# A decoder layer on one core: the first gate and up chunks of the second feed-forward in row form, and seven buffers of converted weights

## The chip, the cores and the metric

The kernel runs on one core of one Trainium2 chip. The metric is the device time of one execution in microseconds (us), from the first to the last instruction and the little that lies around them. Engines are named as the profile names them: PE is TensorE (matmuls and transposes), ACT is ScalarE, DVE is VectorE, POOL is GpSimd, SP is SyncE, which issues nearly all DMAs here.

## The reference

One layer over 256 tokens of width 1024, batch 1: a half feed-forward, a token mixer, a cross-attention to 256 memory tokens, and a second half feed-forward. Each sub-layer normalizes its input, and its output once more before it is added to the residual stream `x`.

```python
def rmsnorm(x, g):
    xf = x.astype(jnp.float32)
    r = lax.rsqrt(jnp.mean(xf * xf, axis=-1, keepdims=True) + RMS_EPS)
    return (xf * r).astype(x.dtype) * g

def swiglu(h, w_gate, w_up, w_down):
    return (jax.nn.silu(h @ w_gate) * (h @ w_up)) @ w_down
...
        h = rmsnorm(x, xa_pre_g[l])
        mem_n = rmsnorm(mem, mem_g[l])
        c = memory_cross_attention(h, mem_n, xa_wq[l], xa_wkv[l], xa_wo[l])
        x = x + rmsnorm(c, xa_post_g[l])

        h = rmsnorm(x, ffn2_pre_g[l])
        f = swiglu(h, ffn2_w_gate[l], ffn2_w_up[l], ffn2_w_down[l])
        x = x + MACARON_WEIGHT * rmsnorm(f, ffn2_post_g[l])
```

The hidden width of the feed-forward is 2816, which is 22 chunks of 128.

## The kernel before

**Products.** Every large product is made of three matmuls on numbers split in a high part (`hi`, rounded for TensorE) and the rest (`lo`): hi by hi, hi by lo, lo by hi. Weights come from HBM in units of 8 tiles of 128 by 128 in the order of use. `Weights._make` converts one unit: ACT casts it to `whi` (L76), DVE subtracts to get `wlo` (L77). `whi` and `wlo` have six buffers each (LEAD + 2), the raw units three buffers of two units. `get` hands out tiles and converts LEAD = 4 units ahead, unless a list `pace` says otherwise for the next units.

**Two forms.** In the column form a tile of weights is the stationary operand and all 256 tokens stream past: the output has features on partitions. `group` is that form for four columns at once, 8 steps k of 12 matmuls of 256 columns (L227, L232, L234). In the row form 128 tokens are the stationary operand and 512 columns of weights stream past: the output has tokens on partitions (`row_product`, L294 to L296).

**The end of a sub-layer (a seam).** `row_end` makes the last three k-steps of the output product (`products`): first the tile of tokens t = 0 in two halves of 512 columns, then t = 1. ACT squares each half (L320), takes the root (L334), DVE inverts it (L335) and adds the normalized half to the residual `xt` (L343). PE then transposes `xt` (L349), 128 by 128 at a time; ACT and DVE split each transposed chunk into the next sub-layer's input, `x_hi` (L370) and `x_lo` (L374). Within a PSUM buffer ACT's and DVE's reads take turns in the order of the program. There are three seams: from the first feed-forward to the mixer, from the mixer to the cross-attention, and from there to the second feed-forward. The first two have fillers, columns of the memory keys (L173 to L175), which PE works on while ACT and DVE finish the tile t = 1; then the next sub-layer's `group` begins. The third has none: `ahead` and `before` thread the transposes of t = 1 through the steps of the `group` that makes the first two gate and up chunks. In a seam all engines follow the written order; outside of it only PE does, and a scheduler orders the others.

**After the third seam.** Chunks 2 to 21 of the feed-forward follow in column form, `gate_up`, with gate in one of the six `acc` buffers of PSUM and up in one of the two `sm` buffers. Between the gate and the up product of chunk 4, `opened` spreads the norm's factors over the partitions: two matmuls into an `sm` buffer (L282, four records in the trace), copied by ACT to `rBx` (L358). Then the chunks made so far are scaled, passed through Silu and split (`finish`). ACT loads a function table when it changes between Sqrt, Exp and Silu.

Of the kernel before, what the change touches and what calls it, by code (L numbers as in the profile page):

```python
# [47 lines left out]
class Weights:  # L48
# [33 lines left out]
    def open_in_parts(self, n_units, load, split):  # L82
# [21 lines left out]
        for c, (raw, hi, lo, parts) in enumerate(steps):  # L104
# [32 lines left out]
def build(nc, io, tiles_only=False):  # L137
# [171 lines left out]
    def row_sums(parts, ks, ws, t, factor, later=None):  # L309
# [54 lines left out]
    def row_end(parts, ks, weights, factor, nxt, pre, fillers):  # L364
# [12 lines left out]
        def products():  # L377
            st["w"].pace = [(LEAD, None)] * (LATE - 1) + [(LEAD - 1, None)]
# [9 lines left out]
            box["sums"] = row_sums(parts, ks, ws, 1, factor, box["later"])  # L388
            x_turn(0, range(4), small)
            x_turn(0, range(4, 8), small)  # L390

        def middle():
            r = box["r"] = row_root(box["sums"])
            if not fillers:
                x_hi(0, 0)
                row_add(1, slice(0, P), r)
                x_hi(0, 1)
                return
            for c in range(ND):
                x_hi(0, c)  # L400
            for i in range(2):
                row_add(1, quarter(i), r)
            box["later"][0]()
            for i in range(2, 4):
                row_add(1, quarter(i), r)
            for c in range(4):
                x_lo(0, c)
# [13 lines left out]
        def ahead():  # L421
            r = box["r"]
            x_turn(1, (0,), accum)
            row_add(1, slice(P, S), r)
            x_lo(0, 0)
            x_turn(1, (1,), accum)
            x_hi(1, 0)
            x_hi(1, 1)
            row_add(1, quarter(1), r)
            x_lo(1, 0)  # L430
            x_lo(0, 1)
            x_lo(1, 1)
            box["later"][0]()

        def before(j):
            if fillers and j == 1:
                k_flush()
            if j == 0 and not fillers:
                st["w"].pace = [(2, "dve"), (2, "pool"), (2, "dve"), (3, "dve"), (3, None), (3, None)]
            if j % 2 == 1 and j < 7 and not fillers:  # L440
                c = j + 1
                x_turn(1, (c, c + 1), accum)
# [662 lines left out]
```

## Time and profile before

| what | us |
|---|---|
| median of 3 runs (lowest to highest) | 579.35 (579.27 to 583.17) |
| the profiled execution | 579.55 |
| its span, first to last instruction | 577.6 |
| PE busy | 566.6 (98%) |
| DVE busy | 406.4 (70%) |
| ACT busy | 342.0 (59%) |
| mean granted TensorE clock, share of 2.4 GHz | 0.996 |

Matmuls are pipelined: the time from the start of one to the start of the next is what it costs, and the duration that a row shows is longer than that. A timeline's row has start, duration, engine, line, operation, output and input tiles, a count where rows are merged, and in brackets the idle time before it with what ended it.

### The profile page before, as it was taken

The numbers are of one execution on the slowest core, as the hardware profiler recorded it, in microseconds if no ns is written. First come the engines' busy times: TensorE is split into PE (matmuls) and PEld (weight loads), VectorE is DVE, ScalarE is ACT, GpSimd is POOL, SyncE is SP. The second block draws the span as 40 slices with busy tenths as digits, with TensorE's granted clock in tenths as the row PEclk, the third lists the DMA queues.
The fourth block names the chain that finished last, engine by engine and source line by source line (L and its number), as shares of the span: only waits on it lengthen the run. The fifth ranks groups of instructions, "written<-read, shape, count | busy, mean of one in ns | idle before, by whom it ended". The sixth has DMA issues, their size and how long they took to land.

```text
span 577.6 us, 8466 instructions
## 1 busy us (share of the span) xinstructions
PE 566.6 (98%) x3288; PEld 494.8 (86%) x3288; DVE 406.4 (70%) x661; ACT 342.0 (59%) x619; POOL 20.0 (3%) x36
## 2 busy tenths in 40 slices
PE   8999999999999999999999999999999999999995
PEld 7888888888888899988899988889888888888884
DVE  5499666778776768985578676468796666676654
ACT  6588675555556565874459466358664555555433
POOL 0000000000000000550000000010000000000001
PEclk9999999999999999999999999999999999999998
DMA  8896575465564247163347625417475455646402
GB/s 270 338 359 220 216 279 216 151 214 166 200 203 165 107 163 280 70 222 142 146 146 253 222 73 164 152 49 266 173 254 195 169 208 162 214 155 210 146 0 74
DMA packets 29832, 107.04 MB, mean 185 GB/s; under 512 B 2144, under 2 KB 3936, under 8 KB 29408
## 3 DMA queue, kind: packets, MB, share of 16 engines
q1 hardware_dynamic: 29360, 105.29, 51.4%
q10 hardware_dynamic: 432, 1.20, 0.6%
q8 instruction: 26, 0.43, 0.3%
q14 instruction: 14, 0.11, 0.1%
HBM read 105.44 MB, written 1.05 MB: 184 GB/s over the span
## 4 chain that ended last, share of the span: by engine, by line
PE 91%; DVE 3%; DMA 3%; ACT 1%; issue 1%; SPq 1%; DVEq 0%; ACTq 0%
PE acc L559 13%; PE sm L559 13%; PE acc L294 10%; PE acc L295 10%; PE acc L296 10%; PE acc L558 6%; PE sm L558 6%; DMA wraw<-w 3%; PE acc L173 3%; PE acc L174 3%; PE acc L175 3%; PE acc L234 2%; PE acc L232 2%; PE acc L260 2%; PE acc L262 2%; PE acc L261 2%
## 5 line engine op out<-in xcount | busy, mean ns | idle before, releaser
L77 DVE TENSOR_TENSOR wlo<-wraw,whi 128x1024 fp32r<-128x1024 f32 x183 | 223.9, 1231 | 84.2 <-ACT whi L76 83.8
L76 ACT CAST whi<-wraw 128x1024 fp32r<-128x1024 f32 x184 | 192.4, 1052 | 54.7 <-PE acc L296 41.4
L559 PE MATMUL acc<-xs,whi 128*128 128x512 f32 x320 | 114.5, 397 | 0.0
L559 PE MATMUL sm<-xs,whi 128*128 128x512 f32 x320 | 114.3, 397 | 0.0
L558 PE MATMUL acc<-xs,wlo 128*128 128x256 f32 x320 | 89.9, 281 | 0.7 <-DVE wlo L77 0.7
L558 PE MATMUL sm<-xs,wlo 128*128 128x256 f32 x320 | 90.0, 281 | 0.0
L559 PEld LDWEIGHTS sm<-xs,whi 128*128 128x128 f32 x320 | 60.1, 188 | 14.8
L559 PEld LDWEIGHTS acc<-xs,whi 128*128 128x128 f32 x320 | 60.1, 188 | 14.3
L294 PE MATMUL acc<-whi,h 128*128 128x512 f32 x176 | 69.7, 396 | 0.0
L295 PE MATMUL acc<-wlo,h 128*128 128x512 f32 x176 | 69.5, 395 | 0.0
L296 PE MATMUL acc<-whi,h 128*128 128x512 f32 x176 | 69.3, 394 | 0.0
L558 PEld LDWEIGHTS acc<-xs,wlo 128*128 128x128 f32 x320 | 60.4, 189 | 2.5 <-DVE wlo L77 1.1
L558 PEld LDWEIGHTS sm<-xs,wlo 128*128 128x128 f32 x320 | 60.5, 189 | 0.0
L173 PE MATMUL acc<-xs,wlo 128*128 128x256 f32 x160 | 46.1, 288 | 0.0
L175 PE MATMUL acc<-xs,whi 128*128 128x256 f32 x160 | 45.2, 283 | 0.0
L174 PE MATMUL acc<-xs,whi 128*128 128x256 f32 x160 | 45.2, 283 | 0.0
L563 ACT COPY cmb<-sm 128x256 f32<-128x256 f32 x40 | 14.9, 372 | 48.4 <-PE sm L559 48.4
L563 ACT COPY cmb<-acc 128x256 f32<-128x256 f32 x40 | 14.9, 372 | 48.1 <-PE acc L559 47.9
L296 PEld LDWEIGHTS acc<-whi,h 128*128 128x128 f32 x176 | 33.0, 187 | 8.1
L295 PEld LDWEIGHTS acc<-wlo,h 128*128 128x128 f32 x176 | 33.0, 188 | 7.8
L294 PEld LDWEIGHTS acc<-whi,h 128*128 128x128 f32 x176 | 33.0, 188 | 6.6
L232 PE MATMUL acc<-xs,whi 128*128 128x256 f32 x128 | 33.6, 292 | 1.0 <-ACT whi L108 1.0
(174 smaller groups left out, 892.5 us busy)
## 6 DMA issues: line engine op xcount, KB each, us to landing
wraw<-w SPq DMA_DIRECT2D x91, 1024.0 KB, 4.8
post<-post SPq DMA_DIRECT2D x4, 512.0 KB, 4.7
wraw<-w SPq DMA_DIRECT2D x7, 256.0 KB, 4.4
wraw<-w SPq DMA_DIRECT2D x2, 512.0 KB, 5.8
xt<-xt ACTq DMA_DIRECT2D x1, 1024.0 KB, 7.3
y<-memt SPq DMA_DIRECT2D x1, 1024.0 KB, 7.8
y<-mem SPq DMA_DIRECT2D x1, 1024.0 KB, 6.9
y<-x SPq DMA_DIRECT2D x7, 128.0 KB, 4.2
```

Of the source, the lines that this page charges most:

```text
L76: self.nc.scalar.copy(hi, raw)
L77: eng.tensor_tensor(lo, raw, hi.bitcast(F32), op=ALU.subtract)
L173: nc.tensor.matmul(o, lo, X[:, :S], start=first, stop=False, skip_group_check=True)
L174: nc.tensor.matmul(o, hi, X[:, :S], start=False, stop=False, skip_group_check=True)
L175: nc.tensor.matmul(o, hi, X[:, S:], start=False, stop=last, skip_group_check=True)
L232: nc.tensor.matmul(o[i], hi, st[X][:, k, :S], start=first and i % 2 == 0, stop=False, skip_group_check=True)
L294: nc.tensor.matmul(o, a, hi, start=first, stop=False, skip_group_check=True)
L295: nc.tensor.matmul(o, a, lo, start=False, stop=False, skip_group_check=True)
L296: nc.tensor.matmul(o, b, hi, start=False, stop=last, skip_group_check=True)
L558: nc.tensor.matmul(ps[:, S:], lo, x[:, :S], start=k == 0, stop=False, skip_group_check=True)
L559: nc.tensor.matmul(ps, hi, x, start=False, stop=k == ND - 1, skip_group_check=True)
L563: nc.scalar.copy(c, ps[:, S:])
```

## The change

It does four things.

1. In the second feed-forward the first two gate and two up chunks are made in row form by `row_group`: 24 matmuls of 512 columns for the tokens t = 0, then 24 for t = 1. All four units of their weights are taken at the start. `row_h` applies the factor, Silu and the product with token rows, and four transposes in `turn_h` bring the result to features on partitions; they stand in `opened`, behind the spread.
2. In all three seams the eight transposes of the tile t = 0 move into the last half of `products`, four behind the first k-step and four behind the second, with three `x_hi` behind the first four.
3. `early` and `late` take the place of `ahead` and the threaded steps: they order ACT's and DVE's work and the transposes of t = 1 around the steps k of the row group. The one conversion on POOL is gone, and `ahead` of `Weights` converts three units between the steps of t = 1.
4. Seven buffers of `whi` and `wlo` instead of six; the reserved memory for descriptors written by an engine is cut to 1024 bytes (no DMA is issued by POOL).

```diff
+    def ahead(self, n):
+        while self.made <= min((self.pos - 1) // UNIT + n, self.n_units - 1):
+            self._make(self.made)
+            self.made += 1
...
             for j, (k, w) in enumerate(zip(ks, ws)):
                 row_product(parts(k), st["acc"], 0, False, j == len(ks) - 1, t, d, w)
+                if (i, j) in between:
+                    between[i, j]()
...
-            box["sums"] = row_sums(parts, ks, ws, 1, factor, box["later"])
-            x_turn(0, range(4), small)
-            x_turn(0, range(4, 8), small)
+            box["sums"] = row_sums(parts, ks, ws, 1, factor, box["later"],
+                                   {(1, i): lambda i=i: turn_first(i) for i in range(2)})
+
+        def turn_first(i):
+            x_turn(0, range(4 * i, 4 * i + 4), small)
+            if i == 0:
+                for c in range(3):
+                    x_hi(0, c)
...
         def middle():
+            if fillers:
+                r = row_root(box["sums"])
+                for c in range(3, ND):
+                    x_hi(0, c)
...
+                return
             for c in range(4):
-                x_lo(0, c)
+                x_lo(0, c) if c < 3 else (x_hi(0, c), x_lo(0, c))
+            box["r"] = row_root(box["sums"])
...
+        def early(k):
+            r = box["r"]
+            if k == 0:
+                for c in range(4, ND):
+                    x_hi(0, c)
+                for i in range(2):
+                    row_add(1, quarter(i), r)
+                x_lo(0, 4)
+                box["later"][0]()
+                for c in range(5, ND):
+                    x_lo(0, c)
+                for i in range(2, 4):
+                    row_add(1, quarter(i), r)
...
+            if k == 6:
+                x_turn(1, range(4), small)
...
+        def late(k):
+            if k == 0:
+                x_turn(1, range(4, 8), small)
...
+            if k in (1, 3, 5):
+                st["w"].ahead(k // 2 + 1)
...
+                for t, ahead in enumerate((early, late)):
+                    for k, (hi, lo) in enumerate(ws):
+                        ahead(k)
+                        a = st[X][:, k, t * P:(t + 1) * P]
+                        b = st[X][:, k, S + t * P:S + (t + 1) * P]
+                        nc.tensor.matmul(ps[t], a, hi, start=k == 0, stop=False)
+                        nc.tensor.matmul(ps[t], a, lo, start=False, stop=False)
+                        nc.tensor.matmul(ps[t], b, hi, start=False, stop=k == ND - 1)
...
         def opened():
             x_spread()
+            if n == 2:
+                turn_h()
...
-              tc.tile_pool(name="hi", bufs=LEAD + 2) as hi,
-              tc.tile_pool(name="lo", bufs=LEAD + 2) as lo,
+              tc.tile_pool(name="hi", bufs=LEAD + 3) as hi,
+              tc.tile_pool(name="lo", bufs=LEAD + 3) as lo,
```

PE at the end of the first seam's `products`, before. L294 to L296 are the three matmuls of a row product, `h` is the hidden layer, L173 is the first filler:

```order
L296 MATMUL acc<-whi,h 128x512
L294 MATMUL acc<-whi,h 128x512
L295 MATMUL acc<-wlo,h 128x512
L296 MATMUL acc<-whi,h 128x512
L349 MATMUL sm<-const,xt 128x128 x8
L173 MATMUL acc<-xs,wlo 128x256
```

The same place of the change, where L300 to L302 are the row product and L357 is the transpose:

```order
L302 MATMUL acc<-whi,h 128x512
L357 MATMUL sm<-const,xt 128x128 x4
L300 MATMUL acc<-whi,h 128x512
L301 MATMUL acc<-wlo,h 128x512
L302 MATMUL acc<-whi,h 128x512
L357 MATMUL sm<-const,xt 128x128 x4
L300 MATMUL acc<-whi,h 128x512
L301 MATMUL acc<-wlo,h 128x512
L302 MATMUL acc<-whi,h 128x512
L179 MATMUL acc<-xs,wlo 128x256
```

The eight transposes stood behind the last product and now stand ahead of its last two k-steps; the other two seams have the same rows.

ACT ahead of and in the first seam, before: L579 is the Silu of chunk 21, L188 the cast of its hidden layer, L615 the load of the Sqrt table, L320 the squares and L334 the root:

```order
L76 CAST whi<-wraw 128x1024
L579 ACTIVATE gu<-gu 128x256
L76 CAST whi<-wraw 128x1024
L188 CAST h<-gu 128x256
L615 ACT_TABLE_LOAD
L76 CAST whi<-wraw 128x1024
L320 ACTIVATE q,fs<-acc 128x512 x2
L334 ACTIVATE fs<-fs 128x1
L320 ACTIVATE q,fs<-acc 128x512 x2
L334 ACTIVATE fs<-fs 128x1
```

The same place of the change, where L683 loads the Sqrt table, L602 is Silu's, L328 the squares and L342 the root:

```order
L76 CAST whi<-wraw 128x1024
L683 ACT_TABLE_LOAD
L602 ACT_TABLE_LOAD
L602 ACTIVATE gu<-gu 128x256
L76 CAST whi<-wraw 128x1024
L194 CAST h<-gu 128x256
L328 ACTIVATE q,fs<-acc 128x512 x2
L342 ACT_TABLE_LOAD
L342 ACTIVATE fs<-fs 128x1
L328 ACTIVATE q,fs<-acc 128x512
L378 ACTIVATE xs<-sm,gain 128x128 x3
L328 ACTIVATE q,fs<-acc 128x512
```

The load of the Sqrt table moved ahead of the last Silu, so that Silu's table is loaded again behind it, and Sqrt's once more between the squares and the first root.

PE between gate and up of chunk 4 in the second feed-forward, before, where L558 and L559 are the products:

```order
L558 MATMUL acc<-xs,wlo 128x256
L559 MATMUL acc<-xs,whi 128x512
L282 MATMUL pb<-const,rcx 128x128 x2
L558 MATMUL sm<-xs,wlo 128x256
L559 MATMUL sm<-xs,whi 128x512
```

And in the change:

```order
L581 MATMUL acc<-xs,wlo 128x256
L582 MATMUL acc<-xs,whi 128x512
L288 MATMUL pb<-const,rcx 128x128 x2
L649 MATMUL ht<-const,hrow 128x128 x4
L581 MATMUL sm<-xs,wlo 128x256
L582 MATMUL sm<-xs,whi 128x512
```

The four transposes `ht` came in behind the spread `pb`. Both take one of the two `sm` buffers, so that the up product behind them gets the buffer of `pb`.

## Rows read from the trace of the kernel before

**Rows 1.** The page's first part, PE: busy time, share of the span, instructions.
```profile
PE 566.6 (98%) x3288; PEld 494.8 (86%) x3288; DVE 406.4 (70%) x661; ACT 342.0 (59%) x619; POOL 20.0 (3%) x36
```
**Rows 2.** The waits of PE: for whom, us in total, times, longest.
```profile
PE acc L349 <- DVE xt L343: 0.9, 1, 0.9
...
PE acc L234 <- DVE xs L374: 0.5, 2, 0.3
```
**Rows 3.** The stretches, third seam: us; PE, PEld, DVE, ACT, POOL busy; PE clock.
```profile
381.21:396.15 14.94, 13.84 (x114) 13.31 (x112) 10.01 (x26) 12.01 (x32) 2.40 (x1) 1.00 0.20 72
```
**Rows 4.** The chain that ended last, in the first seam: start, us, what.
```profile
195.40 0.03 ACT q L320
...
196.65 0.88 DVE xt L343 x2
...
202.35 1.31 DVE xs L374 x5
```
**Rows 5.** The timeline of PE, first seam.
```profile
188.67 0.39 PE L296 MATMUL acc<-whi,h 128*128 128x512 f32 x1
...
193.81 0.39 PE L294 MATMUL acc<-whi,h 128*128 128x512 f32 x1
...
195.20 1.03 PE L349 MATMUL sm<-const,xt 128*128 128x128 f32 x8
195.99 0.37 PE L173 MATMUL acc<-xs,wlo 128*128 128x256 f32 x1
196.19 0.28 PE L174 MATMUL acc<-xs,whi 128*128 128x256 f32 x1
...
203.71 0.39 PE L234 MATMUL acc<-xs,whi 128*128 128x256 f32 x1 [0.25 <-DVE xs L374]
```
**Rows 6.** The timeline of PE, third seam.
```profile
379.84 0.39 PE L294 MATMUL acc<-whi,xs 128*128 128x512 f32 x1
...
381.21 1.03 PE L349 MATMUL sm<-const,xt 128*128 128x128 f32 x8
```
**Rows 7.** The timeline of DVE, third seam.
```profile
378.84 1.41 DVE L343 SCALAR_TENSOR_TENSOR xt<-y,fs,xt 128x512 f32<-128x512 f32 x2
```
**Rows 8.** The timeline of ACT, end of the first feed-forward and first seam.
```profile
181.73 1.05 ACT L76 CAST whi<-wraw 128x1024 fp32r<-128x1024 f32 x1
183.05 0.42 ACT L579 ACTIVATE gu<-gu 128x256 f32<-128x256 f32 x1 [0.27 <-DVE gu L576]
184.20 1.05 ACT L76 CAST whi<-wraw 128x1024 fp32r<-128x1024 f32 x1 [0.74 <-PE acc L296]
...
191.21 0.60 ACT L320 ACTIVATE q<-acc 128x512 f32<-128x512 f32 x1 [1.42 <-PE acc L296]
```
**Rows 9.** The timeline of DVE, the same place.
```profile
186.43 0.42 DVE L189 TENSOR_TENSOR h<-gu,h 128x256 fp32r<-128x256 f32 x1
...
192.53 0.15 DVE L335 RECIPROCAL fs<-fs 128x1 f32<-128x1 f32 x1
192.72 1.42 DVE L343 SCALAR_TENSOR_TENSOR xt<-y,fs,xt 128x512 f32<-128x512 f32 x2
```
**Rows 10.** The timeline of ACT, last rows of the kernel.
```profile
567.06 0.60 ACT L320 ACTIVATE q<-acc 128x512 f32<-128x512 f32 x1 [1.41 <-PE acc L296]
...
567.76 1.28 ACT L334 ACT_TABLE_LOAD   x1
569.06 0.29 ACT L334 ACTIVATE fs<-fs 128x1 f32<-128x1 f32 x1
```
**Rows 11.** The timeline of DVE, last rows of the kernel.
```profile
569.39 0.16 DVE L335 RECIPROCAL fs<-fs 128x1 f32<-128x1 f32 x1 [0.92 <-ACT fs L334]
```
**Rows 12.** The timeline of PE, chunk 4 of the second feed-forward.
```profile
410.29 0.61 PE L282 MATMUL pb<-const,rcx 128*128 128x128 f32 x4
410.65 0.37 PE L558 MATMUL sm<-xs,wlo 128*128 128x256 f32 x1
```
**Rows 13.** The timeline of ACT, chunk 4 of the second feed-forward.
```profile
411.71 0.37 ACT L358 COPY rBx<-pb 128x256 f32<-128x256 f32 x1
```

More of the change, by code (lines that the diff above doesn't have):

```diff
@@ L307, in row_step, with row_sums @@
                 row_product(X, st["acc"], k, first, False, t, d, w)
-    def row_sums(parts, ks, ws, t, factor, later=None):
+    def row_sums(parts, ks, ws, t, factor, later=None, between={}):
         ys = st["ys"]
@@ L419, in turned @@
             return run
[L421 to L433, printed above, removed]
         def before(j):
-            if fillers and j == 1:
+            if j == 1:
                 k_flush()
[L438 to L442, printed above, removed]
-                for k in (c, c + 1):
-                    x_hi(0, k)
-                    x_hi(1, k)
-                if c < 6:
-                    row_add(1, quarter(c // 2 + 1), box["r"])
-                for k in (c, c + 1):
-                    x_lo(0, k)
-                    x_lo(1, k)
@@ L458, in row_end @@
             pr.add(turned(i))
-        if not fillers:
-            pr.add(ahead)
-        return before
+        return before if fillers else (early, late)
     def start():
@@ L588, in opened, with row_group, run, row_h @@
             x_spread()
+            if n == 2:
+                turn_h()
             for f, t in enumerate(early):
-                finish(f, t)
+                finish(f + (2 if n == 2 else 0), t)
+        def row_group(early, late):
+            def run():
+                st["w"].pace = [(3 - i, None) for i in range(4)]
+                ws = [st["w"].get(4) for _ in range(ND)]
+                ps = [accum() for _ in range(2)]
+                for t, ahead in enumerate((early, late)):
[6 more added lines that the diff above has]
+                        nc.tensor.matmul(ps[t], b, hi, start=False, stop=k == ND - 1)
+                st["rows"] = ps
+            pr.add(run, [(n, k * P, c * P) for k in range(ND) for n in (wg, wu) for c in range(2)])
+        def row_h():
+            st["hrow"] = []
+            for t, ps in enumerate(st["rows"]):
+                r = st["rx"][:, t:t + 1]
+                g = st["ffn"].tile([P, S], F32, name="hrow", bufs=2)
+                nc.scalar.activation(g, ps[:, :S], AF.Silu, scale=r)
+                nc.vector.scalar_tensor_tensor(g, ps[:, S:], r, g, op0=ALU.mult, op1=ALU.mult)
+                st["hrow"].append(g)
+        def turn_h():
+            ps = small("ht")
+            for c in range(2):
+                for t in range(2):
+                    nc.tensor.transpose(ps[:, c * S + t * P:c * S + (t + 1) * P],
+                                        st["hrow"][t][:, c * P:(c + 1) * P], st["ident"])
+            for c in range(2):
+                h = st["h", c] = st["ffn"].tile([P, 1, 2 * S], F32R, name="h", bufs=LAG + 4)
+                split_plain(h, 0, ps[:, c * S:(c + 1) * S])
         def down(k):
@@ L595, in down @@
             pr.add(lambda: row_step(st["h", k], 0, k == 0), [(wd, k * P, c * P) for c in range(ND)])
-        group([wg, wu] * 2, X, [0, 0, P, P], early.extend, before=before, hi_first=n == 1)
+        if n == 1:
+            group([wg, wu] * 2, X, [0, 0, P, P], early.extend, before=before, hi_first=True)
+        else:
+            row_group(*before)
         seam(False)
+        if n == 2:
+            side(row_h)
         if n == 1:
@@ L603, in ffn @@
             pr.add(*gate)
-            if f == 3:
+            if f == 3 and n == 1:
                 side(x_root)
```

37 lines of the change are left out of this document (23 added, 14 removed).

## Prediction

> **What bounds the kernel now.** I read the page's busy times first: PE works in 98% of the span [rows 1], so only less work for PE or less waiting of PE can make the kernel faster, and whatever makes PE wait makes it slower by as much. The waits of PE come next: at the third seam PE waits once, 0.9 us, for DVE's addition to `xt` before it can transpose the tile t = 1; at the first and second seam it waits 0.25 us each for `x_lo` of that tile [rows 2, 5]. Then the stretch of the third seam: from the end of the products (381.21) to the start of chunk 2 (396.15) it takes 14.94 us, 1.10 of them without a matmul, at the full clock [rows 3]. Last, the chain of waits through the first seam: it leaves PE with the square of the last half (195.40), runs over the root to DVE's additions (196.65) and from there through DVE alone, up to five `x_lo` that end at 203.66; PE's matmul starts at 203.71 and had idled for it [rows 4, 5]. The reader is to see that at the first two seams the time from the last product to that matmul is DVE's, without a gap that could take in a delay.
>
> **The third seam.** A row product costs 0.228 us: six of them lie between 379.84 and 381.21 [rows 6]. Eight transposes cost 0.79 us and the slow start of the matmul behind them 0.08 (195.20 to 195.99, then 0.20 instead of 0.12), so 0.87 [rows 5]. The new order has on PE, over the same stretch, 48 row products (10.94) and sixteen transposes (1.74), so 12.68 us against 14.94: 2.26 less. That holds if nothing is late, and I went through it with the durations of the rows. The transposes moved into the products need the first half of `xt`, which DVE has at 379.55 (half of 1.41 behind 378.84), while PE comes to them at 379.84: no wait [rows 6, 7]. Behind the products the additions to t = 1 start 1.45 us later in the first seam (195.20 to 196.65 [rows 4, 5]); here one `x_hi` and one `x_lo` stand ahead of them, some 0.35 us more, so 1.8. Two additions take 0.88, an `x_lo` 0.26, the delayed scaling about 0.6, the next `x_lo` 0.35: it is there at 3.9 us. PE wants it as the stationary operand of the third matmul of step k = 5, so after 17 matmuls, 3.88 us. I put a wait of 0.25 there; its ends are 0 and 0.9, the wait that stands there now. Later steps have more room: the last conversion that chunk 2 needs follows the transposes of t = 1 by some 5 us and PE takes 5.5 to get there. The gain is **2.0 us** (1.3 to 2.3).
>
> **Four transposes more.** `turn_h` costs PE half of the eight, **0.44**. Behind it the up product of chunk 4 takes the PSUM buffer of `pb`, which ACT must have copied to `rBx`; before, it took the other one and PE went on at once (410.65 [rows 12]). ACT can start when `pb` has ended (410.90), and the copy takes 0.37 [rows 12, 13], so until 411.27; PE is through with `pb` and `ht` at about 411.0. That is a new wait of **0.3**. If ACT is in the middle of a cast, as it was before when the copy started only at 411.71, it is 1.1; the order has the casts behind the copy now, so I stay at the low end.
>
> **The eight transposes of the first and second seam.** They cost PE the same as before. But they stood behind the last product, where PE had the fillers to go on with and ACT and DVE were at the root already; now they stand ahead of it, so the last half ends 0.87 us later, and the whole chain over DVE with it. DVE's order in the chain is the same, two conversions in it included, and the three `x_hi` taken out were ACT's, not DVE's. PE comes to its matmul at the same time as before and waited there already. So PE waits 0.87 longer, at each of the two: **1.74**. Below that lies nothing only if the chain got shorter; I see no row for that, so the ends are 1.0 and 1.9.
>
> **The tables at the first seam.** The Sqrt load stands ahead of the last Silu now, so there are two loads ahead of it and a third between the squares and the first root. The pattern of the third stands at the end of the kernel: square at 567.06, load of 1.28, reciprocal at 569.39, so 2.33 us [rows 10, 11]; without the load it is 1.32 (191.21 to 192.53 [rows 8, 9]). The root is 1.01 later, since DVE has work of its own meanwhile, and the first half of `xt` is there at 192.72 + 1.01 + 0.71 = 194.44. PE wants to transpose it behind the first k-step, at 193.81 [rows 5, 9]. That is a wait of about **0.7** with the load of the operand (0.3 to 1.0), and it is a pure loss: everything behind it is late too. The two loads ahead of the Silu are hidden, but hardly: ACT's cast ends at 182.78, Silu would start at 185.35 instead of 183.05, 2.30 later; the 0.74 that the next cast waits for a buffer goes away with the seventh one [rows 8]. So the low part of the hidden layer, done at 186.85 before [rows 9], is there at about 188.4; PE wants it at 188.67 [rows 5]. If that cover is gone, each 0.1 counts.
>
> The Trainium skill has a dearer price (ScalarE: Activation LUTs, "What ACT_TABLE_LOAD costs"): a switch is the load of 1283 ns and about 1380 ns of draining. Here the load agrees, but the root starts 0.02 us behind the load's end [rows 10], which leaves no room for a drain. By the page's figure the two early loads would add 2.8 us, an estimate, 2.5 of them beyond the cover, and the third 1.4, so that the sum would be 3.9 us higher.
>
> **What costs nothing.** Casts and subtractions move by one unit because of the seventh buffer, POOL loses its conversion, `row_h` and the split of two chunks take the place of `finish` for them. All of that lies on ACT (59% busy) and DVE (70%) beside chunks on which PE works [rows 1]; without that cover a conversion is 1.05 on ACT. The DMAs are the same in number and order.
>
> **The sum.** -2.0 + 0.44 + 0.3 + 1.74 + 0.7 = +1.2 us on the profiled execution's 579.55 (its span is 577.6), which is 0.2 over the median; I predict a median of **580.5**, a little slower and within 1%. A measurement of this kernel can tell about 1%, 5.8 us, from no change.
>
> **Rivals.**
> - *The seams don't pay.* If the late halves of the first two seams and the tables were hidden, the sum would be -2.0 + 0.44 + 0.3 = -1.3, so 578.1. For it speaks that ACT's `x_hi` are fewer behind the root; against it, that PE already waits at the end of DVE's chain at both places [rows 2, 5]. 13%.
> - *A load holds ACT for longer than its row.* If each held it twice its 1.28, the two early ones would add 2.6, 2.3 of them beyond the 0.3 of cover, and the third 1.3: 3.6 more, 584.1, slower but still within 1%. Its condition is a gap behind a load, and the end of the kernel shows none [rows 10]. 5%. The Trainium skill's draining, on the page named above, is such a gap; by its figure it would be 584.4.
> - *The clock falls.* The first seam gets two waits of PE within 10 us, 0.7 and 1.1. If after them the granted clock fell from 2.4 to 1.2 GHz, PE would do half as much in that stretch. It is slower by over 1% if that stretch lasts 9.4 us or more (half of it is the 4.7 that are missing to 585.2). Against it: the third seam's 1.10 without a matmul left the clock at 1.00 [rows 3]. 3%.
> - *The row group waits at most steps.* If `x_lo` came late by 0.9 for t = 0 and again for t = 1, the gain would be 0.5 and the time 582.0. The room that I count is small at k = 4 and 5 only. 7%.
>
> **How the numbers follow.** The forecast has 70%, with 579.4 to 581.6 as its own range (gain 1.3 to 2.3, seams 1.0 to 1.9, tables 0.3 to 1.0, spread 0.3 to 1.1, not all at one end); 2% is for what I don't see. The range of 8 in 10 reaches into the first and the last rival: 578.5 to 582.3. Faster by over 1% would need three times the third seam's gain: 1%. Slower by over 1% is the clock and a part of the loads: 4%. The rest, 95%, is within 1%.
>
> **What the next profile would show.** Right: the stretch from the end of the products to chunk 2 at the third seam lasts about 12 us, the eight transposes ahead of its start included in the products; PE's waits for `x_lo` at the first and second seam are about 1.1 us instead of 0.25; a wait of PE for `xt` of 0.7 in the first seam's products; a short wait of PE for `rBx` behind `ht`. Wrong: no longer wait at the two seams (then DVE's chain had room that I missed), a wait of PE for the hidden layer ahead of the first seam's third k-step, a third seam with waits at many steps of the row group, or a granted clock under 1.00 behind the first seam.

## The result, and the profile after

The changed kernel is slower: a median of 582.87 us against 579.63 for the kernel before on the same chip, a ratio of 1.0051 [1.0035, 1.0067], so 2.0 to 3.9 us more. It was compared with it twice again while the experiments ran, on two chips: 1.0016 [0.9999, 1.0034] and 1.0053 [1.0033, 1.0074]. I had forecast 580.5, 1.2 more, with 582.3 as the upper end. The side was right, the median lies outside the range, and by the three ratios the cost may not be one number. Both need a cause.

| | before | after |
|---|---|---|
| median (lowest to highest) | 579.63 (578.28 to 583.50) | 582.87 (579.33 to 587.32) |
| the profiled execution, its span | 579.55, 577.6 | 581.94, 580.2 |
| mean granted clock | 0.996 | 0.997 |

Of the 20 executions of after, the eleven with a mean granted clock of 0.997 or more have a median of 581.94, the nine below it one of 583.34.

The page's first part, of the kernel after, answers [rows 1]:

```profile
PE 565.6 (97%) x3244; PEld 492.3 (85%) x3244; DVE 405.8 (70%) x659; ACT 343.9 (59%) x621; POOL 17.4 (3%) x35
```

PE is busy for 1.0 us less in a span that is 2.6 us longer: the loss is waiting. The waits of PE say where (for whom, us in total, times, longest); they answer [rows 2]:

```profile
PE acc L240 <- DVE xs L382: 2.2, 2, 1.1
PE ht L649 <- DVE gu L587: 1.8, 1, 1.8
...
PE sm L581 <- ACT rBx L366: 1.0, 1, 1.0
PE sm L357 <- issue: 0.6, 1, 0.6
```

L240, L357, L382, L366 and L581 are the lines that were L234, L349, L374, L358 and L558. The first line is the two seams with fillers, 1.1 each where 0.25 stood; the last but one and the last were forecast too, if smaller in one case; the wait for `ht`, 1.8, was not. (The rows left out are the start of the kernel, and stand there before as well.)

To see what each place costs I read six rows of PE in every trace, **marks** that both kernels have: A, the first spread of the norm's factors (`pb`); B and C, the first matmul of L234/L240 behind the first and the second seam's chain; D, `pb` of chunk 4; E, the first matmul of chunk 4's up product; F, the last matmul. The timeline of PE of the kernel before (B, D and E are in [rows 5, 12]):

```profile
34.48 0.61 PE L282 MATMUL pb<-const,rcx 128*128 128x128 f32 x4
...
296.07 0.39 PE L234 MATMUL acc<-xs,whi 128*128 128x256 f32 x1 [0.25 <-DVE xs L374]
...
570.82 0.39 PE L296 MATMUL acc<-whi,h 128*128 128x512 f32 x1
```

and of the kernel after, A to F, with the row of the first seam's transposes ahead of B:

```profile
34.25 0.61 PE L288 MATMUL pb<-const,rcx 128*128 128x128 f32 x4
...
194.37 0.63 PE L357 MATMUL sm<-const,xt 128*128 128x128 f32 x4 [0.62 <-issue]
...
205.17 0.39 PE L240 MATMUL acc<-xs,whi 128*128 128x256 f32 x1 [1.12 <-DVE xs L382]
...
298.73 0.39 PE L240 MATMUL acc<-xs,whi 128*128 128x256 f32 x1 [1.11 <-DVE xs L382]
...
410.77 0.61 PE L288 MATMUL pb<-const,rcx 128*128 128x128 f32 x4
413.15 0.66 PE L649 MATMUL ht<-const,hrow 128*128 128x128 f32 x4 [1.78 <-DVE gu L587]
414.77 0.38 PE L581 MATMUL sm<-xs,wlo 128*128 128x256 f32 x1 [0.96 <-ACT rBx L366]
...
573.43 0.40 PE L302 MATMUL acc<-whi,h 128*128 128x512 f32 x1
```

What a stretch takes longer than in the first trace of before is the difference of two marks there less the same difference here: for A to B (205.17 - 34.25) - (203.71 - 34.48) = 1.69. Two more traces of after and one of before come from the experiments.

| stretch | forecast | after | after_again | after_third | before_again |
|---|---|---|---|---|---|
| start to A | 0 | -0.23 | +0.85 | -0.42 | +0.13 |
| A to B, first seam | +1.57 | +1.69 | +1.66 | +1.67 | -0.01 |
| B to C, mixer and second seam | +0.87 | +1.20 | +1.19 | +1.20 | -0.01 |
| C to D, third seam | -2.0 | -2.18 | -2.16 | -2.18 | +0.02 |
| D to E, chunk 4 | +0.74 | +3.64 | +1.49 | +2.93 | 0.00 |
| E to F, the rest | 0 | -1.51 | -1.52 | -1.51 | 0.00 |
| start to F | +1.2 | +2.61 | +1.51 | +1.69 | +0.13 |

Three kinds of rows: the seams repeat to 0.03 us and lie near the forecast; E to F repeats as well and was not forecast; the start and chunk 4 differ from one execution to the next, the start in before as well (the last section), chunk 4 by 2.15 us. Chunk 4 is the step that failed.

**Chunk 4 in the trace of after.** The timeline of ACT, which evacuates PSUM, casts weights and copies `pb` in one queue:

```profile
405.88 0.36 ACT L586 COPY cmb<-acc 128x256 f32<-128x256 f32 x1
410.46 1.05 ACT L76 CAST whi<-wraw 128x1024 fp32r<-128x1024 f32 x1 [4.21 <-DMA wraw<-w]
411.41 0.37 ACT L586 COPY cmb<-sm 128x256 f32<-128x256 f32 x1
411.68 1.05 ACT L76 CAST whi<-wraw 128x1024 fp32r<-128x1024 f32 x1
413.13 1.05 ACT L76 CAST whi<-wraw 128x1024 fp32r<-128x1024 f32 x1 [0.41 <-DMA wraw<-w]
414.08 0.37 ACT L586 COPY cmb<-acc 128x256 f32<-128x256 f32 x1
414.34 0.38 ACT L366 COPY rBx<-pb 128x256 f32<-128x256 f32 x1
```

The cast at 410.46 waits 4.21 us for its weights at the head of the queue. Behind it stands the evacuation of chunk 3's up product (411.41); DVE, which makes the low part of that cast first, finishes the evacuation at 413.1, and only then `ht` gets its `sm` buffer (413.15). Three instructions on, two of them casts, `pb` is copied, and only then the up product of chunk 4 gets the other one (414.77). The chain of waits goes through the same place (start, us, what):

```profile
398.55 5.41 DMA wraw<-w
...
405.19 7.92 DMA wraw<-w
```

The second of these transfers lands at 413.11. It is the one that the cast at 413.13 waits for, and the copy of `pb` stands behind that cast too.

Why the transfer is late shows in the stretches of 4 us (after the times: PE, PEld, DVE, ACT, POOL busy, PE clock, share and GB/s of DMA). Before:

```profile
388.00:392.00 4.00, 4.00 (x36) 4.00 (x35) 1.76 (x6) 3.25 (x9) 2.40 (x1) 1.00 0.11 8
392.00:396.00 4.00, 4.00 (x35) 4.00 (x35) 3.26 (x7) 3.96 (x10) 0.00 (x0) 1.00 0.66 260
396.00:400.00 4.00, 4.00 (x25) 3.53 (x24) 3.92 (x5) 3.44 (x6) 0.00 (x0) 1.00 0.82 266
```

After:

```profile
388.00:392.00 4.00, 4.00 (x23) 3.35 (x22) 2.87 (x10) 2.15 (x9) 0.00 (x0) 1.00 0.00 0
392.00:396.00 4.00, 4.00 (x20) 3.29 (x19) 2.42 (x6) 2.66 (x7) 0.00 (x0) 1.00 0.00 0
396.00:400.00 4.00, 4.00 (x24) 3.46 (x23) 2.53 (x3) 3.95 (x6) 0.00 (x0) 1.00 0.20 17
```

With the conversions halted, the raw buffers stay full and DMA stands still. Before, ACT's first cast in the third seam starts at 387.23 and transfers run again just ahead of 392; after, it starts at 393.61 and they run again just ahead of 400. The casts come 6.4 us later, and `pb` of chunk 4 only 0.5 later, so they have 5.9 us less ahead of it. ACT then casts unit after unit, and from 403.98 on it waits for weights instead of weights for it (0.24 there, then 4.21). That is the theory that the experiments had to test.

### The profile page after: what moved, and what is told of

It reads as the page before. It is cut to its first block, busy times and chain, and to the rows that moved or that the text cites. A ratio compares the mean times of both kernels' runs of the same rounds, so it can differ in the third digit from the quotient of the medians.

```text
span 580.2 us, 8358 instructions
## 1 busy us (share of the span) xinstructions
PE 565.6 (97%) x3244; PEld 492.3 (85%) x3244; DVE 405.8 (70%) x659; ACT 343.9 (59%) x621; POOL 17.4 (3%) x35
## 4 chain that ended last, share of the span: by engine, by line
PE 79%; DVE 8%; DMA 6%; ACT 4%; issue 2%; DVEq 0%; SPq 0%
PE sm L582 12%; PE acc L582 11%; PE acc L300 10%; PE acc L302 10%; PE acc L301 10%; PE sm L581 6%; PE acc L581 6%; DMA wraw<-w 5%; DVE wlo L77 3%; ACT whi L76 2%; PE acc L268 2%; PE acc L266 2%; PE acc L267 2%; PE acc L181 1%; PE acc L180 1%
## 5 line engine op out<-in xcount | busy, mean ns | idle before, releaser
L582 PE MATMUL acc<-xs,whi 128*128 128x512 f32 x320 | 113.7, 394 | 0.0
L582 PE MATMUL sm<-xs,whi 128*128 128x512 f32 x320 | 113.5, 394 | 0.0
L581 PE MATMUL sm<-xs,wlo 128*128 128x256 f32 x320 | 89.9, 281 | 1.0 <-ACT rBx L366 1.0
L581 PE MATMUL acc<-xs,wlo 128*128 128x256 f32 x320 | 89.9, 281 | 0.3 <-DVE wlo L77 0.3
L582 PEld LDWEIGHTS acc<-xs,whi 128*128 128x128 f32 x320 | 60.0, 187 | 13.8
L582 PEld LDWEIGHTS sm<-xs,whi 128*128 128x128 f32 x320 | 60.0, 187 | 13.9
L300 PE MATMUL acc<-whi,h 128*128 128x512 f32 x176 | 69.9, 397 | 0.0
L302 PE MATMUL acc<-whi,h 128*128 128x512 f32 x176 | 69.5, 395 | 0.0
L581 PEld LDWEIGHTS acc<-xs,wlo 128*128 128x128 f32 x320 | 60.4, 189 | 2.1 <-DVE wlo L77 0.6
L581 PEld LDWEIGHTS sm<-xs,wlo 128*128 128x128 f32 x320 | 60.5, 189 | 1.2 <-ACT rBx L366 1.2
L180 PE MATMUL acc<-xs,whi 128*128 128x256 f32 x160 | 45.2, 283 | 0.0
L181 PE MATMUL acc<-xs,whi 128*128 128x256 f32 x160 | 45.2, 283 | 0.0
L302 PEld LDWEIGHTS acc<-whi,h 128*128 128x128 f32 x176 | 33.0, 187 | 8.2
L300 PEld LDWEIGHTS acc<-whi,h 128*128 128x128 f32 x176 | 33.1, 188 | 6.4
L179 PEld LDWEIGHTS acc<-xs,wlo 128*128 128x128 f32 x160 | 30.6, 191 | 0.4
```

Source lines behind the costliest of these rows:

```text
L179: nc.tensor.matmul(o, lo, X[:, :S], start=first, stop=False, skip_group_check=True)
L180: nc.tensor.matmul(o, hi, X[:, :S], start=False, stop=False, skip_group_check=True)
L181: nc.tensor.matmul(o, hi, X[:, S:], start=False, stop=last, skip_group_check=True)
L300: nc.tensor.matmul(o, a, hi, start=first, stop=False, skip_group_check=True)
L302: nc.tensor.matmul(o, b, hi, start=False, stop=last, skip_group_check=True)
L581: nc.tensor.matmul(ps[:, S:], lo, x[:, :S], start=k == 0, stop=False, skip_group_check=True)
```

## The experiments

Each is one edit of the changed kernel unless it says otherwise. Ratios are against the kernel before on the same chip. The stretches are those of the table above, against the first trace of before:

| run | start to A | A to B | B to C | C to D | D to E | E to F | median us | ratio |
|---|---|---|---|---|---|---|---|---|
| e1_turns_back | +0.05 | 0.00 | +0.30 | -2.15 | +2.08 | -1.51 | 578.18 | 0.9986 [0.9968, 1.0004] |
| e2_table_order | +0.06 | +0.88 | +1.20 | -2.18 | +1.73 | +0.01 | 580.64 | 1.0009 [0.9994, 1.0025] |
| e2_again | -0.08 | +0.87 | +1.22 | -2.19 | +3.07 | +0.02 | 582.24, one run | |
| e3_early_convert | -0.88 | +1.68 | +1.20 | -2.18 | +1.48 | -1.51 | 580.90 | 1.0013 [0.9995, 1.0031] |
| r_raw4 | +1.86 | +2.28 | +1.17 | -2.18 | +1.48 | -1.51 | 582.22 | 1.0043 [1.0026, 1.0060] |
| b_seven_buffers | -0.94 | -0.01 | +0.31 | +0.01 | 0.00 | +0.01 | 580.00 | 1.0007 [0.9992, 1.0021] |
| e5_ht_acc | +0.30 | +1.68 | +1.20 | -2.19 | +1.50 | +0.01 | 581.83, one run | |
| c1_turns_convert | +0.33 | -0.01 | +0.27 | -2.19 | +1.48 | -1.52 | 577.71 | 0.9955 [0.9940, 0.9969] |
| c2_turns_convert_acc | -0.21 | -0.01 | +0.29 | -2.15 | +0.44 | -1.53 | 576.14 | 0.9928 [0.9916, 0.9940] |

### The transposes behind the products again

```diff
-                                   {(1, i): lambda i=i: turn_first(i) for i in range(2)})
+                                   {} if fillers else {(1, i): lambda i=i: turn_first(i) for i in range(2)})
+            if fillers:
+                x_turn(0, range(4), small)
+                x_turn(0, range(4, 8), small)
...
-                for c in range(3, ND):
+                for c in range(ND):
                     x_hi(0, c)
```

> The changed kernel with one part undone: in the two seams that have fillers (first and second) the eight transposes of the first tile of tokens stand behind the row products again and the rounding of x_hi for that tile is whole in the middle; the third seam stays as changed. Theory (moving them ahead shortens the cover and makes the low parts of x late): the waits of L238/L240 on DVE's low part, 2.2 us in 2, fall to about 0.5, each of the two seams ends 0.9 us earlier, and the time falls by 1.7 us against the changed kernel (about 581.2). Rival (the 0.9 us at each seam has another source, such as PE's products running later): the time stays within 0.4 us of the changed kernel. Both expect the wait for ht at chunk 4 (1.8 us) to stay.

Measured: 578.18. The waits of PE:

```profile
PE acc L240 <- DVE xs L382: 0.5, 2, 0.2
PE ht L652 <- DVE gu L590: 0.3, 1, 0.3
```

A to B is that of before and B to C within 0.3 of it: the theory of the seams is right, and the 0.25 that stood there twice is back. It gives 2.6 us at the seams, more than the 1.7 that I had written, since the wait for the table (0.6 for L357 in after) is in no row of this trace, where no transpose stands inside the products. The comparison gains another 1.6 at chunk 4 (3.64 to 2.08), where this edit changes nothing and where I had expected the wait for `ht` to stay at 1.8: in this trace the cast waited 3.06 for its weights.

### The table's load ahead of the squares

```diff
             st["w"].flush()
+            if nxt == "xs_mix":
+                nc.scalar.preload_act_table(AF.Sqrt)
             st["ys"] = keep([P, 2, D], "y")
...
-        side(lambda: st["w"].defer(lambda: nc.scalar.preload_act_table(AF.Sqrt)))
```

> The changed kernel with the request for the Sqrt table of the first seam written ahead of the squares of the row sums, where the kernel before had its load, instead of behind them. Theory (the load of 1.28 us stands between the squares and the root, and the transposes of PE wait for the root's row 0.6 us): that wait goes and the time falls by 0.7 us against the changed kernel. Rival (the low parts of x are late in any case and take the gain, since the seam ends by DVE's x_lo): the wait of the transposes goes, that of L240 grows by as much, and the time stays.

Measured: A to B loses 0.88 instead of 1.69, so the load's place costs 0.81. In after the load stands between the square and the root, the timeline of ACT:

```profile
191.48 0.19 ACT L328 ACTIVATION_READ_ACCUMULATOR q<-acc 128x1 f32 x1
191.69 1.28 ACT L342 ACT_TABLE_LOAD   x1
192.98 0.29 ACT L342 ACTIVATE fs<-fs 128x1 f32<-128x1 f32 x1
```

and in the variant the root follows the square at once:

```profile
191.77 0.19 ACT L328 ACTIVATION_READ_ACCUMULATOR q<-acc 128x1 f32 x1
191.99 0.29 ACT L342 ACTIVATE fs<-fs 128x1 f32<-128x1 f32 x1
```

The waits of L240 stay at 1.1 each, so the rival (that `x_lo` takes the gain) falls. The Trainium skill's price of a switch (ScalarE: Activation LUTs, "What ACT_TABLE_LOAD costs"), with some 1380 ns of draining on top of the load, is not what these rows show: in after the load starts 0.02 behind the square's last row and the root 0.01 behind the load's end, as at the end of the kernel before [rows 10]. Two things were not expected: chunk 4 was cheaper (D to E +1.73), and E to F lost the 1.5 us that after gains there.

### Conversions drawn forward

```diff
+                st["w"].ahead(1)
                 for i in range(2):
                     rows_square(st["xt"], st["xsum"], i)
...
                     x_lo(1, c)
+                st["w"].ahead(2)
...
                     x_lo(1, c)
+                st["w"].ahead(3)
                 for i in range(2, 4):
...
-            if k in (1, 3, 5):
-                st["w"].ahead(k // 2 + 1)
```

> The changed kernel with the three steps that convert weights ahead in the row group drawn forward: from steps 1, 3 and 5 of the second tile's half to the first step of the first half (ahead of the squares), its step 6, and the first step of the second half. Theory T1 (conversions restart 6 us later than before, the three raw buffers stay full, DMA stands still, and at chunk 4 a cast waits for its transfer at the head of ScalarE's queue with the evacuations behind it): DMA resumes about 5 us earlier, the cast's wait for DMA of 4.2 us near 410 us falls below 1, PE's waits for ht (1.8) and for rBx (1.0) fall below 0.5 each, and the time falls by 2 to 3 us against the changed kernel. Rival T2 (ht shares the two PSUM buffers sm with the gate and up products, and waits for up 3's evacuation in any case): DMA resumes earlier, ht still waits over 1.2 us, the time falls by 1 us at most. A third case: the casts put ahead of the squares and of the second tile's x_hi hold ScalarE and PE waits at the row group instead; then a wait of L629 or L631 shows.

Measured: D to E is 1.48, and PE no longer waits for `ht`. The stretches:

```profile
392.00:396.00 4.00, 4.00 (x20) 3.30 (x19) 3.48 (x8) 4.00 (x8) 0.00 (x0) 1.00 0.64 185
396.00:400.00 4.00, 4.00 (x25) 3.48 (x24) 3.72 (x7) 3.97 (x8) 0.00 (x0) 1.00 0.84 270
```

DMA moves 185 and 270 GB/s where it moved 0 and 17, and no cast of chunk 4 waits for weights. That is what T1 said, and since the PSUM buffers are untouched, T2, by which `ht` waits in any case, falls. What stays is the wait for `rBx`, 0.8, which T1 had below 0.5. The timeline of ACT shows why:

```profile
410.58 1.05 ACT L76 CAST whi<-wraw 128x1024 fp32r<-128x1024 f32 x1
411.52 0.38 ACT L366 COPY rBx<-pb 128x256 f32<-128x256 f32 x1
```

A cast stands ahead of the copy here too, and `pb` waits for it. Neither the seam nor the row group got a wait by the earlier casts. The median fell by less than the 2 to 3 us expected (580.90 against 582.87, not on the same chip); the ratio fell from 1.0051 to 1.0013. This trace is the fastest of the twelve executions (579.13), so it doesn't say what chunk 4 did in the others; c1 below has the same edit and the same 1.48 in a trace at its median.

### A fourth raw buffer

```diff
-              tc.tile_pool(name="raw", bufs=3) as raw,
+              tc.tile_pool(name="raw", bufs=4) as raw,
```

> The changed kernel with four buffers instead of three for weights as they arrive (raw). Theory T1: transfers go one unit further while conversions stand still, the cast near 410 us waits less for its transfer (4.2 us now, under 2.5), the waits of PE for ht and rBx at chunk 4 (2.8 us together) fall below 1.2, and the time falls by 1.5 to 2.5 us against the changed kernel. Rival T2 (PSUM buffer of ht): ht waits as before, the time falls by less than 0.7 us.

Measured: chunk 4 does as T1 says, 1.48, without a wait for `ht`. Yet the time stayed at 582.22. This trace is late at A by 1.86, and the two waits at the start add up to more than in any other trace (2.1 for the first `whi`, 1.7 for the next `wlo`):

```profile
7.06 0.38 PE L238 MATMUL acc<-xs,whi 128*128 128x256 f32 x1 [2.10 <-ACT whi L108]
```

Whether a fourth transfer, which shares the first microseconds with those that PE waits for, has a part in it isn't shown by one trace beside others that vary at the start by 1.8. The 0.6 that A to B has beyond after is not lost in the seam: from A to the next `pb` it takes 45.61 us here (36.34 to 81.95) and 45.00 in after (34.25 to 79.25), and behind that no more. It is the slower of the two paces of the last section.

### The same kernels again

> The changed kernel again, unaltered: a second trace of it. Open is whether the cast's wait for DMA near 410 us (4.2 us in the first trace) and PE's wait for ht (1.8 us) stand in every execution or come and go with the landing of the weights. In the variants e1 and e2, which leave the conversions alone, that wait of ScalarE was 3.06 and 2.77 us, and PE's wait for ht 0.29 and 0. Theory (a late transfer's wait passes on to PE by whatever it exceeds some 2.8 us): the two numbers of this trace lie on that line, ht's wait being the cast's wait less 2.8, or none. Rival (the wait for ht is fixed by the order of instructions of the changed kernel): it is 1.8 again whatever the cast waits. The seam's waits (0.6, 1.1, 1.1) and that for rBx (0.8 to 1.0) repeat by either. The time is 581 to 584.

> The kernel before again, unaltered: a second trace of it. In its first trace the matmuls of 512 columns in the second feed-forward's column chunks start 239 ns ahead of the next instruction, in four of the five traces of the changed kernel and its variants 230 ns. If this belongs to the program, it is 239 here again; if it belongs to the execution, it may be 230, and the time is then about 1.5 us lower (578.0).

> The changed kernel a third time, with more rounds: the first comparison gave 1.0051 of the kernel before, the second 1.0016. Open is whether the cost is one number. If the transfers' landing at chunk 4 and at the start decides (the cast's wait for DMA was 4.21 and 2.54 us in the two traces, PE's wait for ht 1.8 and 0), the ratio lies between the two, 1.001 to 1.005, and the trace's wait for ht is again the excess of the cast's wait over some 2.8 us. If the chance of a run does not decide, the ratio is one of the two again.

> e2_table_order again, unaltered. Its PE instructions are the same as those of the changed kernel, one by one, yet in its trace the 512-column matmuls of the second feed-forward are 240 ns apart from the next instruction, as in both traces of the kernel before, and 230 in the changed kernel. If the spacing belongs to the loaded program, it is 240 again; if it belongs to the execution, 230 may show, and the end is then 1.5 us earlier.

Medians: after 581.05 (ratio 1.0016) and 582.02 (1.0053); before 579.68 in its one run. The two numbers that were asked for, how long ACT's cast waits for its weights near 410 us and how long PE then waits for `ht`:

| trace | cast waits | PE waits for `ht` | difference |
|---|---|---|---|
| after | 4.21 | 1.78 | 2.43 |
| e2_again | 4.12 | 1.33 | 2.79 |
| after_third | 3.98 | 1.20 | 2.78 |
| e1_turns_back | 3.06 | 0.29 | 2.77 |
| e2_table_order | 2.77 | 0 | |
| after_again | 2.54 | 0 | |

Two of them as the timelines have them, after_third:

```profile
409.66 1.05 ACT L76 CAST whi<-wraw 128x1024 fp32r<-128x1024 f32 x1 [3.98 <-DMA wraw<-w]
```
```profile
PE ht L649 <- DVE gu L587: 1.2, 1, 1.2
```

and after_again, whose list of PE's waits has no `ht` at all:

```profile
409.49 1.05 ACT L76 CAST whi<-wraw 128x1024 fp32r<-128x1024 f32 x1 [2.54 <-DMA wraw<-w]
```

PE waits by whatever the cast's wait exceeds 2.78 by. In the first trace it is 0.35 more: the cast at 403.98 had waited 0.24 there, and the cast's long wait began 4.52 us ahead of `pb`, against 4.88 in the other two traces of after. In e2_table_order no wait is listed, yet `ht` starts 0.60 behind `pb`, against 0.44 in after_again. The rival, a wait that the order of instructions fixes, falls: the same program shows 1.8, 1.2 and none. So the cost of the change depends on when one transfer lands. In after_again the cast waited least of the three, and its comparison gave the smallest ratio. The third ratio, 1.0053, is the first again and not between the two, which I had written for the case that chance doesn't decide; whether the chip does isn't shown by one trace on each.

The expectation of 578.0 for before_again didn't come true: its E to F is that of the first trace to 0.01 (see the last section).

### Seven buffers alone, on the kernel before

```diff
-              tc.tile_pool(name="hi", bufs=LEAD + 2) as hi,
-              tc.tile_pool(name="lo", bufs=LEAD + 2) as lo,
+              tc.tile_pool(name="hi", bufs=LEAD + 3) as hi,
+              tc.tile_pool(name="lo", bufs=LEAD + 3) as lo,
...
-    nc = bacc.Bacc("TRN2", target_bir_lowering=False, num_devices=1)
+    nc = bacc.Bacc("TRN2", target_bir_lowering=False, num_devices=1, dynamic_dma_scratch_size=1024)
```

> The kernel before with one part of the change alone: seven buffers of converted weights instead of six, and the smaller scratch for DMA. PE's instructions stay, one by one; casts, low parts and evacuations change places on ScalarE and DVE. By the prediction this costs nothing (the time within 0.5 us of the kernel before). Rival: the casts drawn forward hold evacuations, and a wait of PE for an accumulator or sm shows, or the spacing of the 512-column matmuls changes from 239 to 230 ns and the time falls by 1.5 us.

Measured: 580.00, a ratio of 1.0007 [0.9992, 1.0021], no cost that shows. The trace has one, though: B to C is 0.31 longer, at one place in the mixer, where the transposes of `ps` start 0.36 apart instead of 0.11:

```profile
246.99 0.27 PE L671 MATMUL acc<-const,ps 128*128 128x128 f32 x1
247.35 0.33 PE L669 MATMUL acc<-const,ps 128*128 128x128 f32 x1
```

The same 0.3 stands in every variant with seven buffers, those with the transposes undone too. So of the 1.20 between B and C, 0.9 is the transposes (forecast 0.87) and 0.3 comes with the seventh buffer (or the smaller reserved memory, which this edit has too). What delays the transposes of `ps` I did not follow.

### `ht` in an accumulator

```diff
-            ps = small("ht")
+            ps = accum()
```

> The changed kernel with ht in an accumulator's PSUM buffer instead of one named sm. In c2, where the casts are earlier, this took away the wait for rBx of 0.8 us. Here a cast still waits for its transfer ahead of the evacuation of chunk 3's up products. Theory: the up products of chunk 4 take the buffer that this evacuation frees, so PE waits there by whatever the cast's wait exceeds 2.8 us by, and not for rBx: at a cast's wait of 2.5 no wait of over 0.3 us at chunk 4, at 4.2 one of 1.0 to 1.8. Rival (the buffer alone was at fault): no wait at chunk 4 whatever the cast waits.

Measured: the cast waited 4.04, and PE waits where the theory put it, at the up product, for the evacuation and not for `rBx`:

```profile
411.72 0.60 PE L649 MATMUL acc<-const,hrow 128*128 128x128 f32 x4
413.14 0.39 PE L581 MATMUL sm<-xs,wlo 128*128 128x256 f32 x1 [0.82 <-DVE gu L587]
```

It is 0.82 where I had written 1.0 to 1.8: by the line above 4.04 gives 1.26, and PE is busy with `ht` for 0.44 of it. So the buffer alone was not at fault: the late evacuation costs PE whichever tile comes next. But it had a large part, which I had not written. In after_third the cast waited about as long (3.98), and there D to E is 2.93 against 1.50 here: between these two traces 1.43 us go with the buffer. With `ht` in one of the two named sm, first `ht` waits for the evacuation and then the up product for `rBx`.

### Both, and all three

c1 takes the edits of e1 and e3 together, c2 that of e5 as well.

> The two edits of e1_turns_back and e3_early_convert together, on the changed kernel. If the waits at the seams and the starved conversions are separate causes, the time is that of e1 less the rest of ht's wait (0.3) and less the runs in which the transfer is later: 577.5 to 578, 0.3 to 0.4 per cent below the kernel before. If e1 had already taken what e3 mends, it equals e1 (578.2). The wait for rBx (0.8 to 0.9) stays in either case.

> As c1_turns_convert, and ht takes an accumulator's PSUM buffer instead of one of the two named sm. Theory: the wait of 0.8 to 1.0 us for rBx is there because pb and ht take both sm buffers, so that the up products of chunk 4 stand behind the copy of pb; with ht elsewhere they take the buffer that the up products of chunk 3 left, that wait goes, and the time is 0.7 us below c1. Rival (the evacuations are late as a whole, behind a cast at the head of ScalarE's queue): the wait moves to the gate or up products of chunk 5 or to an accumulator, and the time is that of c1 within 0.2 us.

Measured: 577.71 and 576.14. In c1 the gains add: no loss at the first seam, 0.27 of the seventh buffer, chunk 4 at 1.48 with 0.80 for `rBx`. In c2 that wait is gone and nothing takes its place, the timeline of PE:

```profile
408.21 0.61 PE L288 MATMUL pb<-const,rcx 128*128 128x128 f32 x4
408.66 0.60 PE L653 MATMUL acc<-const,hrow 128*128 128x128 f32 x4
409.01 0.36 PE L585 MATMUL sm<-xs,wlo 128*128 128x256 f32 x1
```

From `pb` to the up product it takes 0.80, against 0.36 before [rows 12]: the four transposes cost 0.44, and that is all that chunk 4 has to cost. D to E falls by 1.04 from c1 to c2, where I had written 0.7. c2 is 0.72% [0.60, 0.84] faster than the kernel before, the fastest of all the kernels here.

## Why the prediction was wrong, step by step

- **The third seam, -2.0.** Right: -2.16 to -2.19 in every trace. The wait of 0.25 that I had added to the computed 2.26 does not stand there. [rows 3] is answered by the stretch from the row group's first matmul to chunk 2, 11.84 us without a wait where I had said about 12:

```profile
384.80:396.64 11.84, 11.84 (x57) 9.80 (x56) 7.58 (x23) 8.44 (x27) 0.00 (x0) 1.00 0.00 0
```

- **The transposes of the first two seams, 0.87 each.** Right: e1 takes them back, and 0.88 and 0.9 are what remains of them at the first seam in e2 and at the second without the buffer's 0.3. The rival that the seams don't pay fell with that.
- **The table at the first seam, 0.7.** Right: 0.81 by e2. The cover of the two early loads held: no trace has a wait for the hidden layer ahead of the third k-step. The rival of a load that holds ACT longer than its row fell, and so did the clock's (0.997) and that of a row group that waits (no wait of PE for it in any trace).
- **Four transposes more, 0.44 + 0.3.** The 0.44 is exact (c2). The wait for `rBx` failed: 1.04 in place of 0.3 (1.48 less 0.44). Of it 0.80 is idle; the rest is the end of the last transpose, which the up product overlaps in c2 (there it starts 0.35 behind `ht`, whose row is 0.60 long). I had the other end, 1.1, in hand and put it aside with the words "the order has the casts behind the copy now". The order of ACT has a cast behind the copy, but also two ahead of it, with the evacuation of the gate product between:

```
L586 COPY cmb<-sm 128x256
L76 CAST whi<-wraw 128x1024 x2
L586 COPY cmb<-acc 128x256
L366 COPY rBx<-pb 128x256
L194 CAST h<-ht 128x256
```

- **"What costs nothing."** This is the step that failed most. I let casts and DMAs off because they are the same in number, and because ACT is busy for 59% only. What had moved is when the casts come: 6.4 us later in the third seam (387.23 to 393.61), with DMA at rest until the first two are through. It comes back at chunk 4 as a cast that waits 2.5 to 4.2 us for its weights with evacuations behind it, 0 to 2.15 us of PE's time (1.49, 2.93 and 3.64 at D to E), the more since `ht` and `pb` hold both `sm` buffers (e5). e3 and r_raw4 take it away from two sides, by earlier casts and by one transfer more in hand. The share of busy time says nothing on that: the instruction that waits is not busy.
- **The rest.** The seventh buffer comes with 0.3 in the mixer (forecast nothing), and E to F is 1.51 shorter (forecast nothing). The sum in the first trace: 1.69 + 1.20 - 2.18 + 3.64 - 1.51 - 0.23 = 2.61. Without the 1.51, whose cause I don't know, the first ratio would be 1.008 instead of 1.005. And after_again, 1.0 above before by the medians, agrees with my +1.2 by luck: that gain sets off the unforeseen losses there. I had also written that a measurement tells about 1% from no change; the intervals here reach 0.2% to either side.

The profiled execution accounts for 2.4 of the loss (581.94 less 579.55). The median of the 20 lies 0.9 above it, which no trace shows. By the list at the result it lies with the executions of a lower granted clock than the traced one's 0.997; none of those was traced, so where they lose it stays open.

## What to carry to other kernels

When a change moves conversions or casts, look at when the transfers behind them run again: a stretch with DMA at 0 GB/s and full buffers can be a debt, paid later by the first instruction that stands ahead of something urgent in an in-order queue. Not every such stretch is paid for: in the kernel before DMA moved nothing from 378 to 391 us and a cast waited 1.25 us for its weights at 400.80, yet no wait of PE followed; in after it moved nothing from 383 to 399, and the cast waited 4.21. Cover found in the program's order has to be read for all that stands ahead of the instruction, not for its neighbour. And a tile that takes a turn in a pool of two buffers makes the next user wait for another tile than before; a wait that the kernel did not have is found by counting the turns.

## What the runs showed of the hardware that I had not expected

**Two paces of the same matmuls.** In the column chunks a matmul of 256 columns (L558/L581) and one of 512 (L559/L582) take turns, and PE waits for nothing. The timelines, first and last start of eight pairs in one product, before:

```profile
422.01 0.28 PE L558 MATMUL acc<-xs,wlo 128*128 128x256 f32 x1
...
424.48 0.28 PE L558 MATMUL acc<-xs,wlo 128*128 128x256 f32 x1
```

and after:

```profile
420.44 0.28 PE L581 MATMUL sm<-xs,wlo 128*128 128x256 f32 x1
...
422.86 0.28 PE L581 MATMUL sm<-xs,wlo 128*128 128x256 f32 x1
```

That is 2.47 and 2.42 us for seven pairs. Over some 245 pairs from 419 us on it is 353.3 ns a pair in six traces (before twice, b_seven_buffers, e2 twice, e5) and 347.1 in eight (after three times, e1, e3, r_raw4, c1, c2), with nothing between, at the same granted clock; it makes the 1.51 us of E to F. A pace holds from one interruption of PE to the next: in all traces but r_raw4, which is at 353 there, the first feed-forward runs at 347 between the `pb` at 34 us and that at 79, and at 353 behind it. From 419 us on a kernel that was run again kept its pace, whether PE had waited for `ht` or not. e2 and after have the same instructions on PE, one by one, and differ in ScalarE's order alone, and e5 and c2 place their PSUM tiles alike; so neither of these sets it. The expectation of before_again that it belongs to the execution fell for this stretch. Between PE's wait for weights near 26 us and the `pb` at 34 us it holds: there before has 346.7 in its first trace and 352.9 in its second, and e2_again 346.7 where e2_table_order has 353.3. So the program alone does not set the pace there, and what sets it stays open.

**The start varies.** Mark A lies between 33.5 and 36.3 us in fourteen traces. PE's waits for the first weights differ from trace to trace, and so does the clock: in the two traces with the latest A, after_again and r_raw4, PE waited 2.0 and 2.1 us for the first `whi`, and behind that the granted clock is 0.50 (1.2 GHz) between 8 and 10 us in the one and between 10 and 12 us in the other. In those 2 us of r_raw4 PE has 11 matmuls, in the same ones of after 17. How much of the spread is whose I did not work out. That is more than most of the terms of my sum, so single executions of this kernel should be compared from a mark on, not from the start.
